# A hybrid decoder trunk: the decays of rows 512 to 1023 in two groups of two heads, and the minimum of their logits on VectorE

## The chip, the cores and the metric

One core of a Trainium2 chip. The metric is the time of one execution in microseconds (us) on the device, as the median of several runs. The engines are TensorE (PE in the profile, with its weight loads as PEld), VectorE (DVE), ScalarE (ACT), GpSimd (POOL) and the queue SP that issues the transfers (DMA). Matmuls write into eight PSUM banks of 128 x 512 fp32.

## The reference

One decoder layer over 1024 rows of 1024 columns. The normed input is projected once, and cut into q, k, v, z_a, a low-rank gate and the parts of a convolution branch. The part that matters here is the decay of the gated linear attention:

```python
gk = log_sigmoid(gk_low @ w_gk2 + b_gk) / 16        # (rows, 4 heads x 128)
b = cumsum(gk, within chunks of 64 rows)
q_in, k_in, k_dec = q * exp(b), k * exp(-b), k * exp(b_last - b)
```

With z = gk_low @ w_gk2 + b_gk, the log-sigmoid is min(z, 0) - ln(1 + exp(-|z|)). Beside it stand v, which the attention sums up, and z_a, which goes through Silu into a gate.

## The kernel before

Each wide projection (512 output columns for each 512-row half, with a contraction of 1024) is made of seven smaller products in the manner of Strassen. `wide` (L1339) takes two such blocks of columns, v and then za. Of each it runs products 3, 1, 2, 5, 4, 6 in this order, each 4 contraction tiles by 4 row blocks by 3 matmuls (the values are split into a high and a low fp32r part, `mm3`, L609): 48 matmuls of 128 x 512. Product 3 ends in four accumulators X; products 1 and 5 go into four accumulators V; products 2, 4 and 6 into Y. X and Y lie in the banks `first`, V in the banks `second`. For za, `first` is m4, m5 and two of the kind o, and `second` is m0 to m3. V is read by VectorE after product 5 (`zau <- zaV`), Y after product 4 (`zas <- zaY`).

The weights of a product are prepared by VectorE and ScalarE: raw tiles are loaded (`zaraw`, later q0raw, k0raw, q1raw, k1raw, all in 8 common buffers), combined (`zaT`), cast to the high part on ScalarE (`za6hi <- zaT`) and subtracted for the low part on VectorE (`za6lo`).

Into these products the kernel weaves side work, a step after each few matmuls (`weave`, `tick`, `finish_woven`, L617 to L632). Of it:

- `low_rank(half)` (L1513) makes the low-rank gate of one half of the rows, in a bank and then in a tile `low`.
- `decays(half, tags)` (L1534) does for each of four heads one matmul into a bank (`zp`), and from that bank two ScalarE operations: Relu(-z - b) into `c`, with a negated bias `nbgk`, and Abs(z + b) into `t`. Then follow Exp and Ln in place for all four heads, and for each head on VectorE the sum of both, a scan over the rows of a chunk, a subtraction and a tiny product (`dds`); scan and subtraction are stored.
- `quarter_sums(1)` (L1565) makes sums of the activations (`qs`), split and stored to `tqd`; they are loaded again later as `turned0h` and `turned0l` for the cells of q and k, in the matmuls `k0X <- turned0h` and `q0X <- turned0h`.
- `weights` prepares the weights of later projections (`wt`).

`extra` (L1604) runs the decays of rows 0 to 511 within v's products, through the argument `late` of `wide`, a function that `wide` calls ahead of product 4. `more` (L1610) runs those of rows 512 to 1023, in the banks m0 to m3, and `quarter_sums(1)` behind them; it is woven from the start of za on.

The order of the instructions isn't that of the code. All operations are recorded; each gets a due time, worked backward over what depends on it with estimated costs (`set_dues`, L373), and a list scheduler (`put_in_order`, L420) then takes, for each engine, the earliest due of those that are ready by its clock. The matmuls of the products stay in their order; side matmuls such as `zp` go in where their operands are ready and a bank is free. `emit` (L501) then issues everything, so all instructions have the line L508, and they are told apart by their names. Each engine runs its instructions in order, and so does SP; each transfer also waits for the one that is eight places before it.

Of the kernel before, what the change touches and what calls it, by code (L numbers as in the profile page):

```python
# [9 lines left out]
F32 = mybir.dt.float32  # L10
# [3 lines left out]
AF = mybir.ActivationFunctionType  # L14
ALU = mybir.AluOpType

P = 128
D = 1024
SEQ = 1024
HALF = 512  # L20
H = 4
DV = 256
CH = 64
NP = HALF // P
# [495 lines left out]
def kernel(  # L520
# [16 lines left out]
    nc = Flow(tc)  # L537
    PS = bass.MemoryType.PSUM
    tt = nc.vector.tensor_tensor
    stt = nc.vector.scalar_tensor_tensor  # L540
    act = nc.scalar.activation
# [21 lines left out]
    bgk = vec[:, 0:4]  # L563
# [8 lines left out]
    def dram(name, *shape):  # L572
        return dr.tile([P, *shape], F32, name=name)
# [5 lines left out]
    cd = [[[dram(f"c{w}d{h}_{i}", HALF) for w in "cd"] for i in range(2)] for h in range(H)]  # L579
# [16 lines left out]
    store = nc.sync.dma_start  # L596
# [6 lines left out]
    def mm(*a, **kw):  # L603
        nc.tensor.matmul(*a, skip_group_check=True, **kw)
# [12 lines left out]
    def weave(gen, after=1):  # L617
        woven.append([after, gen])
# [11 lines left out]
    def finish_woven():  # L630
        while woven:
            tick()  # L632
# [334 lines left out]
    def pairs(cs):  # L967
        for c in cs:
            c.prods = [k for k in PAIR if k in c.prods]
        return [list(cs[n:n + 2]) for n in range(0, len(cs), 2)]  # L970

    def run_groups(groups, more=(), ahead=6):


        todo = line_up(groups)
        seq = todo + line_up(more)
        for n, (c, k) in enumerate(todo):
            for reach, what in ((RING + ahead, "load"), (RING - 1, "prep")):
                met = set()
                for cc, kk in seq[n:]:  # L980
                    if cc not in met:
                        reach -= cc.slots
                    if cc.slots > 1:
                        met.add(cc)
                    if reach < 0 or not cc.ready(kk):
                        break
                    getattr(cc, what)(kk)
            c.run(k)
# [488 lines left out]
    with phase("v", [ph["prep0"]]) as qp:  # L1477
# [14 lines left out]
        smask = qp.tile([P, HALF], F32, name="smask")  # L1492
# [14 lines left out]
        nc.scalar.copy(g2, g2raw)  # L1507
        tt(g2[64:128], g2raw[64:128], f(g2[64:128]), op=ALU.subtract)
        lows = {}
        nbgk = qp.tile([P, 4], F32, name="nbgk")  # L1510
        nc.vector.tensor_scalar(nbgk, bgk, -1.0, None, op0=ALU.mult)

        def low_rank(half):  # L1513

            ops = ((0, 0), (4, 3)) if half == 0 else ((0, 1), (8, 6))
            glx = qp.tile([P, 8, 4, 32], F32R, tag="wt", name=f"glx{half}")
            for n, (g0, _) in enumerate(ops):
                nc.scalar.copy(glx[:, 4 * n:4 * n + 4], f(glw[:, g0:g0 + 4, None, :].to_broadcast([P, 4, 4, 32])))
            lowp = pso.tile([P, 512], F32, tag="o", name=f"lowp{half}", bufs=2)
            n = 0  # L1520
            for g0, k in ops:
                for kt in range(4):
                    gl = glx[:, n // 2].rearrange("p a b -> p (a b)")
                    for s in range(2):
                        nc.apart = 0.0 if n else 1.0
                        mm(lowp, gl, hres[k][s][:, kt, :], start=n == 0, stop=n == 15)
                        n += 1
            low = qp.tile([P, 512], F32R, tag="low", name=f"low{half}")
            nc.scalar.copy(low, lowp)
            for a in (32, 96):  # L1530
                tt(low[a:a + 32], lowp[a:a + 32], f(low[a:a + 32]), op=ALU.subtract)
            lows[half] = low

        def decays(half, tags):  # L1534
            t1 = [qp.tile([P, HALF], F32, tag="t1", name=f"t1_{half}{h}", bufs=4) for h in range(H)]
            c = [qp.tile([P, HALF], F32, tag="c4", name=f"c4_{half}{h}", bufs=4) for h in range(H)]
            for h in range(H):
                zp = pso.tile([P, 512], F32, tag=tags[h], name=f"zp{half}_{h}", bufs=2 if tags[h] == "o" else 1)
                cs = slice(h * P, (h + 1) * P)
                nc.apart = 1.0  # L1540
                mm(zp, g2[:, cs], lows[half], start=True, stop=True)
                nc.apart, nc.hurry = 0.0, 6.0
                act(c[h], zp, AF.Relu, scale=-1.0, bias=nbgk[:, h:h + 1])
                act(t1[h], zp, AF.Abs, bias=bgk[:, h:h + 1])
                nc.hurry = 0.0
                yield 1
            for t in t1:
                act(t, t, AF.Exp, scale=-1.0)
            for t in t1:
                act(t, t, AF.Ln, bias=1.0)  # L1550
            yield 1
            by = lambda t: t.rearrange("p (n c t) -> p n c t", c=2, t=CH)
            for h in range(H):
                tt(t1[h], t1[h], c[h], op=ALU.add)
                nc.vector.tensor_tensor_scan(c[h], smask, t1[h], 0.0, op0=ALU.mult, op1=ALU.add)
                store(cd[h][half][0], c[h])
                last = by(c[h])[:, :, :, CH - 1]
                tt(by(t1[h]), by(c[h]), by(c[h])[:, :, :, CH - 1:CH].to_broadcast([P, NP, 2, CH]), op=ALU.subtract)
                store(cd[h][half][1], t1[h])
                dc = dcs[:, h, half]  # L1560
                act(dc, last, AF.Exp, scale=-1 / 16.0)
                tt(dds[:, h, half], dc[:, :, 0], dc[:, :, 1], op=ALU.mult)
                yield 1

        def quarter_sums(k):  # L1565


            hi, lo = (f(t) for t in hres[k])
            at = lambda t, i, j: t[:, 2 * i:2 * i + 2, 256 * j:256 * j + 256]

            def tile(n):
                return qp.tile([P, 512], F32, tag="c4", name=f"qs{k}{n}", bufs=4).rearrange("p (a b) -> p a b", a=2)

            def apart(n, a, b):
                t, o = tile(n), tile("o")
                tt(t, at(hi, *a), at(hi, *b), op=ALU.subtract)
                tt(o, at(lo, *a), at(lo, *b), op=ALU.subtract)
                tt(t, t, o, op=ALU.add)
                return t

            def less(n, a, t):
                o = tile(n)
                tt(o, at(hi, *a), t, op=ALU.subtract)
                tt(o, o, at(lo, *a), op=ALU.add)
                return o

            def put(n, src):
                hl = [qp.tile([P, 512], F32, tag="t1", name=f"qs{k}{n}{w}", bufs=4).rearrange("p (a b) -> p a b", a=2) for w in "hl"]
                split(*(t.bitcast(F32R) for t in hl), src)
                for w, t in enumerate(hl):  # L1590
                    store(tqd[k][n][w], t)

            t = apart(0, (0, 1), (0, 0))
            put(0, t)
            yield 2
            t = less(1, (1, 1), t)
            put(1, t)
            yield 2
            put(3, less(3, (1, 0), t))
            yield 2  # L1600
            put(2, apart(2, (1, 1), (0, 1)))
            yield 2

        def extra():  # L1604
            low_rank(0)
            yield 2
            yield from decays(0, ("o",) * 4)
            low_rank(1)

        def more():  # L1610
            yield from decays(1, ("m0", "m1", "m2", "m3"))
            yield from quarter_sums(1)

        wide("v", [wv[0, n] for n in range(4)], v_cons, ("m0", "m1", "m2", "m3"), ("o", "o", "m4", "m5"),
             [(ep, "ev", 3)] * 2, [(ep, "ev", 3), (qp, "t1", 4)], begun, lambda: weave(extra(), 1))
        weave(more(), 1)
        weave(weights(qp, pieces[:3], 3, 5.0), 2)
        wide("za", [wv[1, n] for n in range(4)], z_cons, ("m4", "m5", "o", "o"), ("m0", "m1", "m2", "m3"),
             [(qp, "vhi", 2)] * 2, [(qp, "vlo", 2)] * 2)
        finish_woven()  # L1620
        qks = []
        for hp in range(2):
# [367 lines left out]
    with phase("late", [ph["sw"], ep]) as lp:  # L1990
# [57 lines left out]
        with phase("fin", [ph["sw4"]], lp) as gp:  # L2048
# [152 lines left out]
            last = pairs(gts)  # L2201
# [74 lines left out]
```

## Time and profile before

| what | value |
|---|---|
| median of 3 runs | 1072.09 us (1071.81 to 1072.77) |
| profiled execution | 1072.38 us |
| its span in the trace | 1070.5 us |
| mean granted TensorE clock | 0.998 |
| ScalarE table loads | 20, 1283 ns each |
| transfers | 262.06 MB |

In the lines of a timeline stand the start in us from the start of the span, the length, the engine, and the instruction with its tiles as output <- inputs, numbers left out; at the end in brackets the idle time of the engine ahead of it and whom it waited for. Lines that overlap are pipelined: the distance between two starts, the pitch, is what an instruction costs in a row of them. A line of the waits has the waiting instruction, the one waited for, the sum in us, how often, and the longest. A window has busy time and count of PE, PEld, DVE, ACT and POOL, the granted clock, the DMA share and GB/s. A group of a line has the total busy time and the mean ns. For a transfer the last number is the median time from issue to landing.

### The profile page before, as it was taken

What the parts mean: (1) busy time and instruction counts of PE and PEld (TensorE: products, weight loads), DVE (VectorE), ACT (ScalarE), POOL (GpSimd) and SP (SyncE); (2) the same over time, 40 slices, a digit from 0 to 9 for tenths busy, and PEclk for the clock granted to TensorE, in tenths of its full rate; (3) what the DMA queues carried; (4) which work ended last, traced back from release to release, by engine and by line L of the source; (5) the groups of instructions that cost most, each with busy time, mean ns of one, the idle gap of its engine ahead of it and who ended that gap; (6) DMA issues with size and microseconds to landing.
All of it is one profiled execution on the core that took longest, in us unless ns stands there. A gap on an engine that the chain in (4) does not pass through costs nothing.

```text
span 1070.5 us, 15921 instructions
## 1 busy us (share of the span) xinstructions
PE 1059.7 (99%) x5175; PEld 896.3 (84%) x5175; DVE 917.5 (86%) x1553; ACT 662.8 (62%) x1241; POOL 45.4 (4%) x83
## 2 busy tenths in 40 slices
PE   9999999999999999999999999999999999999996
PEld 7888887888888888888888888888888888888886
DVE  6889768977997888889889788887999879889896
ACT  6866689856654544566556376765856635466555
POOL 0000000000000000000000011110000000012021
PEclk9999999999999999999999999999999999999999
DMA  9985578785867443654557779978586779799973
GB/s 313 330 316 174 187 231 307 260 285 200 257 213 244 154 152 130 215 173 154 197 180 243 247 241 346 324 275 322 199 305 229 284 220 312 244 328 337 300 235 133
DMA packets 166979, 262.06 MB, mean 245 GB/s; under 512 B 14448, under 2 KB 79728, under 8 KB 163952
## 3 DMA queue, kind: packets, MB, share of 16 engines
q1 hardware_dynamic: 166752, 260.79, 72.1%
q8 instruction: 40, 0.66, 0.2%
q14 instruction: 43, 0.35, 0.1%
q10 hardware_dynamic: 144, 0.26, 0.1%
HBM read 168.72 MB, written 92.27 MB: 244 GB/s over the span
## 4 chain that ended last, share of the span: by engine, by line
PE 98%; ACT 1%; DMA 1%; DVE 0%; issue 0%; SPq 0%; POOL 0%; POOLq 0%; ACTq 0%
PE vY L508 3%; PE zaY L508 3%; PE vV L508 2%; PE op L508 2%; PE zaV L508 2%; PE pe L508 2%; PE zaX L508 1%; PE vzV L508 1%; PE vzX L508 1%; PE kv L508 1%; PE ga1Y L508 1%; PE ga0Y L508 1%; PE k0Y L508 1%; PE zc2Y L508 1%; PE zc1Y L508 1%; PE ga2Y L508 1%
## 5 line engine op out<-in xcount | busy, mean ns | idle before, releaser
L508 DVE TENSOR_TENSOR wt<-wt 128x256 f32<-128x256 f32 x64 | 26.9, 420 | 2.2 <-DMA wtd<-wt 1.9
L508 ACT ACT_TABLE_LOAD x20 | 25.7, 1283 | 1.1 <-PEq L2265 0.7
L508 DVE SCALAR_TENSOR_TENSOR u<-t,vec,u 128x512 f32<-128x512 f32 x32 | 23.8, 747 | 2.6 <-ACT u L508 2.5
L508 ACT ACTIVATE junk<-x 128x512 bf16<-128x512 f32 (+1 forms) x30 | 18.0, 600 | 12.0 <-DVE x L508 11.7
L508 POOL MEMSET t<- 128x2 f32 x8 | 0.8, 100 | 410.3 <-ACT kk L508 206.5
L508 POOL TENSOR_SCALAR rg<-ms 128x1 f32<-128x1 f32 x8 | 6.4, 798 | 261.6 <-ACT junk L508 261.4
L508 ACT ACTIVATE u<-t,vec 128x512 f32<-128x512 f32 x16 | 11.6, 726 | 7.9 <-issue 4.6
L508 ACT ACTIVATE junk<-op 128x256 bf16<-128x256 f32 x32 | 12.2, 380 | 3.8 <-PE op L508 3.7
L508 ACT ACTIVATE wt<-wt,vec 128x256 f32<-128x256 f32 x32 | 13.6, 497 | 1.0 <-DMA wt<-in_wb_dram 1.0
L508 ACT ACTIVATE og<-op,or 128x256 f32<-128x256 f32 x32 | 13.3, 470 | 1.2 <-POOL or L508 1.1
L508 ACT CAST S<-S 128x512 fp32r<-128x512 f32 x14 | 8.6, 617 | 8.7 <-PE op L508 7.5
L508 PE MATMUL pe<-wpehi,pThi 128*128 128x512 f32 x32 | 12.7, 398 | 0.6 <-ACT pThi L508 0.5
L508 ACT ACTIVATE oq<-oq,vec 128x512 f32<-128x512 f32 x20 | 13.1, 715 | 0.0
L508 PE MATMUL op<-v,aTh 128*128 128x256 f32 x64 | 12.8, 283 | 0.0
L508 PE MATMUL pe<-wpelo,pThi 128*128 128x512 f32 x32 | 12.7, 398 | 0.0
L508 DVE TENSOR_TENSOR szl<-og,szl 128x512 f32<-128x512 f32 x16 | 11.0, 687 | 2.0 <-ACT og L508 2.0
L508 PE MATMUL pe<-wpehi,pTlo 128*128 128x512 f32 x32 | 12.1, 393 | 0.0
L508 POOL TENSOR_TENSOR or<-or,mhalf 128x2 f32<-128x2 f32 x16 | 11.9, 746 | 1.3
L508 DVE SCALAR_TENSOR_TENSOR hq<-hq,vec,rt 128x512 f32<-128x512 f32 x16 | 11.4, 741 | 0.0
L508 DVE TENSOR_TENSOR s<-y,s 128x512 f32<-128x512 f32 x16 | 11.0, 686 | 0.5 <-ACT s L508 0.5
L508 POOL TENSOR_SCALAR or<-oms 128x2 f32<-128x2 f32 x16 | 5.6, 348 | 137.6 <-ACT junk L508 137.6
L508 DVE TENSOR_TENSOR x<-x,pe 128x512 f32<-128x512 f32 (+1 forms) x18 | 11.2, 629 | 0.3
(3671 smaller groups left out, 4333.7 us busy)
## 6 DMA issues: line engine op xcount, KB each, us to landing
wtd<-wt SPq DMA_DIRECT2D x88, 128.0 KB, 2.7
wt<-in_wb_dram SPq DMA_DIRECT2D x16, 512.0 KB, 4.5
v<-vd SPq DMA_DIRECT2D x16, 512.0 KB, 5.9
wgq<-wtd SPq DMA_DIRECT2D x7, 1024.0 KB, 6.6
qk<-qkd SPq DMA_DIRECT2D x12, 512.0 KB, 6.0
vraw<-in_wv_dram SPq DMA_DIRECT2D x20, 256.0 KB, 3.3
zaraw<-in_wv_dram SPq DMA_DIRECT2D x20, 256.0 KB, 4.4
uq<-ud SPq DMA_DIRECT2D x5, 1024.0 KB, 6.9
```

The costliest lines, as they stand in the source:

```text
L508: o.call(*[place(a) for a in o.args], **{k: place(a) for k, a in o.kw.items()})
```

## The change

In `decays`, VectorE adds the bias and takes the minimum with 0 in one operation that reads the bank, in place of ScalarE's Relu of the negated logit; the later sum becomes a difference. The negated bias isn't made any more. This holds for both halves of the rows. `decays` also gets the heads as an argument: of rows 512 to 1023 heads 0 and 1 stay in `more`, now in m0 and m1, and heads 2 and 3 are run in m2 and m3 by the function that `wide` calls ahead of za's product 4, when V has been read out of these banks.

```diff
-        nbgk = qp.tile([P, 4], F32, name="nbgk")
-        nc.vector.tensor_scalar(nbgk, bgk, -1.0, None, op0=ALU.mult)
...
-        def decays(half, tags):
-            t1 = [qp.tile([P, HALF], F32, tag="t1", name=f"t1_{half}{h}", bufs=4) for h in range(H)]
-            c = [qp.tile([P, HALF], F32, tag="c4", name=f"c4_{half}{h}", bufs=4) for h in range(H)]
-            for h in range(H):
+        def decays(half, heads, tags):
+            t1 = [qp.tile([P, HALF], F32, tag="t1", name=f"t1_{half}{h}", bufs=4) for h in heads]
+            c = [qp.tile([P, HALF], F32, tag="c4", name=f"c4_{half}{h}", bufs=4) for h in heads]
+            for n, h in enumerate(heads):
...
-                act(c[h], zp, AF.Relu, scale=-1.0, bias=nbgk[:, h:h + 1])
-                act(t1[h], zp, AF.Abs, bias=bgk[:, h:h + 1])
+                nc.vector.tensor_scalar(c[n], zp, bgk[:, h:h + 1], 0.0, op0=ALU.add, op1=ALU.min)
+                act(t1[n], zp, AF.Abs, bias=bgk[:, h:h + 1])
...
-                tt(t1[h], t1[h], c[h], op=ALU.add)
+                tt(t1[n], t1[n], c[n], op=ALU.subtract)
...
-            yield from decays(0, ("o",) * 4)
+            yield from decays(0, range(4), ("o",) * 4)
             low_rank(1)
 
         def more():
-            yield from decays(1, ("m0", "m1", "m2", "m3"))
+            yield from decays(1, range(2), ("m0", "m1"))
             yield from quarter_sums(1)
...
-             [(qp, "vhi", 2)] * 2, [(qp, "vlo", 2)] * 2)
+             [(qp, "vhi", 2)] * 2, [(qp, "vlo", 2)] * 2, None, lambda: weave(decays(1, range(2, 4), ("m2", "m3")), 1))
```

The order that the scheduler makes changes with it, up to about a third of the program; behind that the two orders are the same. Three places follow. In the rows a number behind a name tells tiles of one name apart; zp_2 and zp_3 are the decays' matmuls of heads 2 and 3.

TensorE at the end of za's product 3 and the start of product 1 (zaV), before:

```order
757 L508 MATMUL zaX_1815<-za3hi_1822,h3hi 128x512
758 L508 MATMUL zaX_1815<-za3lo_1847,h3hi 128x512
759 L508 MATMUL zaX_1815<-za3hi_1822,h3lo 128x512
760 L508 MATMUL zaV_2000<-za1hi_1864,h1hi 128x512
761 L508 MATMUL zp_3_2004<-low_1742,g_1407 128x512
762 L508 MATMUL zaV_2000<-za1lo_1880,h1hi 128x512
763 L508 MATMUL zaV_2000<-za1hi_1864,h1lo 128x512
764 L508 MATMUL zaV_2014<-za1hi_1864,h1hi 128x512
```

The last zp of rows 512 to 1023 stood within the first row block of V, and zp_2 eight rows ahead of it. Now TensorE has them a third into product 4 (zaY), which follows product 5:

```order
909 L508 MATMUL zaY_2028<-za4hi_2161,h4hi 128x512
910 L508 MATMUL zaY_2028<-za4lo_2193,h4hi 128x512
911 L508 MATMUL zaY_2028<-za4hi_2161,h4lo 128x512
912 L508 MATMUL zp_2_2374<-low_1759,g_1407 128x512
913 L508 MATMUL zaY_2086<-za4hi_2161,h4hi 128x512
914 L508 MATMUL zp_3_2382<-low_1759,g_1407 128x512
915 L508 MATMUL zaY_2086<-za4lo_2193,h4hi 128x512
```

Both stand around the fourth row block of the first contraction tile, after 9 and 10 of the 48 matmuls of product 4. On VectorE, what empties the banks ahead of them and reads them stands in this order now (zau empties V, c_12 and c_13 are the new operations of heads 2 and 3):

```order
267 L508 TENSOR_TENSOR k0T_2326<-k0raw_2225,k0raw_2217 128x512
268 L508 TENSOR_TENSOR qs12l<-qs_2263,qs12h 128x512
269 L508 TENSOR_TENSOR za6lo_2340<-zaT_1587,za6hi_2334 128x512
270 L508 TENSOR_TENSOR zau_2214<-zaV_1989,zau_2214 128x512
271 L508 TENSOR_TENSOR q0k00S_2351<-q0raw_2173,k0raw_2217 128x256
272 L508 TENSOR_TENSOR zau_2229<-zaV_1999,zau_2229 128x512
273 L508 TENSOR_TENSOR zau_2237<-zaV_2011,zau_2237 128x512
274 L508 TENSOR_TENSOR zau_2251<-zaV_2019,zau_2251 128x512
275 L508 TENSOR_SCALAR c_12_2380<-zp_2_2374,vec 128x512
276 L508 TENSOR_SCALAR c_13_2387<-zp_3_2382,vec 128x512
```

The four zau stand together, the third and fourth of them empty m2 and m3; before, the order had two of them ahead of the four zas and two behind the zas. Eleven rows later the first subtraction of head 2 (`t_12 <- t_12, c_12`) stands directly ahead of the four zas. The third place is SP, where the turned activations are loaded, now:

```order
220 L508 DMA q1raw_2531<-in_wc_dram 128x512
221 L508 DMA k1raw_2559<-in_wc_dram 128x512
222 L508 DMA q1raw_2566<-in_wc_dram 128x512
223 L508 DMA k1raw_2570<-in_wc_dram 128x512
224 L508 DMA q1raw_2577<-in_wc_dram 128x512
225 L508 DMA turned0h<-tqd_1h 128x512
226 L508 DMA turned0l<-tqd_1l 128x512
```

Before, only the first q1raw load and a store of zau stood ahead of these; four more loads do now. On ScalarE the eight Relu are gone, and there are three table loads more, since Exp and Ln of heads 2 and 3 now come apart from those of heads 0 and 1.

More of the change, by code (lines that the diff above doesn't have):

```diff
@@ L1532, in low_rank @@
             lows[half] = low
-        def decays(half, tags):
-            t1 = [qp.tile([P, HALF], F32, tag="t1", name=f"t1_{half}{h}", bufs=4) for h in range(H)]
-            c = [qp.tile([P, HALF], F32, tag="c4", name=f"c4_{half}{h}", bufs=4) for h in range(H)]
-            for h in range(H):
-                zp = pso.tile([P, 512], F32, tag=tags[h], name=f"zp{half}_{h}", bufs=2 if tags[h] == "o" else 1)
+        def decays(half, heads, tags):
+            t1 = [qp.tile([P, HALF], F32, tag="t1", name=f"t1_{half}{h}", bufs=4) for h in heads]
+            c = [qp.tile([P, HALF], F32, tag="c4", name=f"c4_{half}{h}", bufs=4) for h in heads]
+            for n, h in enumerate(heads):
+                zp = pso.tile([P, 512], F32, tag=tags[n], name=f"zp{half}_{h}", bufs=2 if tags[n] == "o" else 1)
                 cs = slice(h * P, (h + 1) * P)
@@ L1552, in decays @@
             by = lambda t: t.rearrange("p (n c t) -> p n c t", c=2, t=CH)
-            for h in range(H):
-                tt(t1[h], t1[h], c[h], op=ALU.add)
[L1555 to L1559, printed above, removed]
+            for n, h in enumerate(heads):
+                tt(t1[n], t1[n], c[n], op=ALU.subtract)
+                nc.vector.tensor_tensor_scan(c[n], smask, t1[n], 0.0, op0=ALU.mult, op1=ALU.add)
+                store(cd[h][half][0], c[n])
+                last = by(c[n])[:, :, :, CH - 1]
+                tt(by(t1[n]), by(c[n]), by(c[n])[:, :, :, CH - 1:CH].to_broadcast([P, NP, 2, CH]), op=ALU.subtract)
+                store(cd[h][half][1], t1[n])
                 dc = dcs[:, h, half]
```

## The prediction

> **What bounds the kernel.** I read the page first (engine shares, chain), then the waits of the whole run, then the timelines of TensorE and ScalarE around the one wait that matters. From the page, the span, the engines' busy time and the chain that ended last:
>
> ```profile
> span 1070.5 us, 15921 instructions
> PE 1059.7 (99%) x5175; PEld 896.3 (84%) x5175; DVE 917.5 (86%) x1553; ACT 662.8 (62%) x1241; POOL 45.4 (4%) x83
> PE 98%; ACT 1%; DMA 1%; DVE 0%; issue 0%; SPq 0%; POOL 0%; POOLq 0%; ACTq 0%
> ```
>
> TensorE is busy for 99% of the span and is 98% of the chain. So a change of the other engines' work is worth only the time in which TensorE waits. These are all of TensorE's waits in the run (total, times, longest):
>
> ```profile
> PE zaV L508 <- ACT t L508: 1.2, 2, 1.0
> PE warm L508 <- DVE zero L508: 1.0, 1, 1.0
> PE pe L508 <- ACT pThi L508: 0.5, 1, 0.5
> ```
>
> The last two lie at the start, where nothing is edited. The first is the place of the change. TensorE's timeline there (start, length, instruction; zp is the fourth head's decay matmul):
>
> ```profile
> 178.33 0.39 PE L508 MATMUL zp<-low,g 128*128 128x512 f32 x1
> ...
> 179.49 0.40 PE L508 MATMUL zaV<-za1hi,h1lo 128*128 128x512 f32 x1
> 180.86 0.50 PE L508 MATMUL zaV<-za1hi,h1hi 128*128 128x512 f32 x1 [0.98 <-ACT t L508]
> 181.20 0.40 PE L508 MATMUL zaV<-za1lo,h1hi 128*128 128x512 f32 x1
> 181.44 0.40 PE L508 MATMUL zaV<-za1hi,h1lo 128*128 128x512 f32 x1
> 182.02 0.51 PE L508 MATMUL zaV<-za1hi,h1hi 128*128 128x512 f32 x1 [0.18 <-ACT t L508]
> 182.36 0.40 PE L508 MATMUL zaV<-za1lo,h1hi 128*128 128x512 f32 x1
> ```
>
> And ScalarE's in the same microseconds:
>
> ```profile
> 178.08 1.58 ACT L508 ACTIVATE sz<-zaX 128x512 f32<-128x512 f32 x3
> 179.53 0.70 ACT L508 ACTIVATE c<-zp,nbgk 128x512 f32<-128x512 f32 x1
> 180.10 0.71 ACT L508 ACTIVATE t<-zp,vec 128x512 f32<-128x512 f32 x1
> 180.67 0.72 ACT L508 ACTIVATE c<-zp,nbgk 128x512 f32<-128x512 f32 x1
> 181.24 0.73 ACT L508 ACTIVATE t<-zp,vec 128x512 f32<-128x512 f32 x1
> ```
>
> Row block 2 of V needs bank m2, which holds the third head's zp until its Abs (`t<-zp`, 180.10) has read it; row block 3 needs m3, held until the Abs at 181.24. Both stand behind three Silu of `sz` and the Relu (`c<-zp`). TensorE follows each Abs at once.
>
> **What goes.** The undisturbed pitch of a matmul comes from two anchors, the first matmul of product 5 and the first of product 6, 96 matmuls apart; the third head's zp stands with them:
>
> ```profile
> 176.48 0.39 PE L508 MATMUL zp<-low,g 128*128 128x512 f32 x1
> ...
> 201.88 0.39 PE L508 MATMUL zaV<-za5hi,h5hi 128*128 128x512 f32 x1
> ...
> 223.64 0.39 PE L508 MATMUL zaY<-za6hi,h6hi 128*128 128x512 f32 x1
> ```
>
> (223.64 − 201.88)/96 = 0.227 us. From 179.49 to 182.36 there are 5 steps in 2.87 us, where 5 × 0.227 = 1.13 would do: **1.74 us** lost. After the change heads 2 and 3 aren't in m2 and m3 at all at this time. Were the banks free? The zp of heads 2 and 3 themselves started in them at 176.48 and 178.33 without waiting, and V wants them no earlier than 179.7, so what used them before is gone 1.4 us or more ahead. The whole 1.74 us goes at this place; no other wait of TensorE is near the edit, so nothing more than that can be gained.
>
> **What is added, and its cover.** Eight Relu leave ScalarE (8 × 0.57, the pitch of 179.53 to 180.10, = 4.6 us), three table loads come. Eight VectorE operations from a bank come, a small one (nbgk) leaves. The trace has no such TENSOR_SCALAR. Its bounds are the two-input operation from the bank (0.69 long, 0.60 from one to the next) and, below, the 128x256 operation (0.42 long); I take 0.60, since the bank and the 512 columns are those of the first row. Neither engine is on the chain, so these cost nothing as long as the following cover holds. VectorE, from the `vs` that ends its long wait at 149.77 to the first `zau` (window, then rows and groups):
>
> ```profile
> 149.77:216.51 66.74, 65.58 (x286) 53.23 (x285) 61.30 (x104) 60.59 (x101) 0.00 (x0) 1.00 0.81 270
> ```
>
> ```profile
> 216.51 0.69 DVE L508 TENSOR_TENSOR zau<-zaV,zau 128x512 f32<-128x512 f32 x1
> ...
> 221.99 1.88 DVE L508 TENSOR_TENSOR zas<-zaY,zas 128x512 f32<-128x512 f32 x3
> ```
>
> ```profile
> L508 DVE TENSOR_TENSOR_SCAN c<-smask,t 128x512 f32<-128x512 f32 x8 | 9.8, 1219 | 0.0
> ...
> L508 DVE TENSOR_TENSOR wt<-wt 128x256 f32<-128x256 f32 x12 | 5.1, 421 | 0.0
> ```
>
> The pitch is (1.88 − 0.69)/2 = 0.60, so 0.09 less than the length; for the scan 1.13, for `wt` 0.33. Between these two points the new order lacks the later work of heads 2 and 3 (2 × (0.60 + 1.13 + 0.60) = 4.7), three `wt` (1.0) and one za3lo (0.6), together 6.3; it has two new bank operations, q0T, k0T and a qs12l in addition, 5 × 0.60 = 3.0. Busy time 61.3 − 3.3 = 58.0, so the first `zau` starts at 207.8 with no idle time, and at 213.2 with the same 5.4 us idle as before.
>
> What it must meet: zp of head 2 now stands in TensorE's order nine matmuls into product 4, in m2, and V's third block in m2 is released by the third `zau`. Product 5 starts at 201.88 − 1.74 − 0.45 (two zp gone from ahead) = 199.69; zp of head 2 is due 57 × 0.227 = 12.9 later, **212.6**. On the way to the first `zau` VectorE waits for the third cast of za6, whose buffer product 5 must have read. ScalarE's rows:
>
> ```profile
> 210.24 0.62 ACT L508 CAST za6hi<-zaT 128x512 fp32r<-128x512 f32 x1 [1.46 <-PE zaV L508]
> ...
> 215.94 0.62 ACT L508 CAST qs12h<-qs 128x512 fp32r<-128x512 f32 x1
> 216.58 1.28 ACT L508 ACT_TABLE_LOAD   x1
> 217.87 1.15 ACT L508 ACTIVATE zau<-zau 128x512 f32<-128x512 f32 x2
> ```
>
> That is 8.36 after product 5's start, so 208.05 now; with the cast (0.62) and za6lo (0.60) the first `zau` is at **209.3**, between the two ends, and nearer to the lower one. The third ends 2.2 later (0.60 + 0.33 + 0.60 + 0.69), at 211.5, the fourth at 212.1. Cover: 1.1 us at zp of head 2, 1.0 at head 3's.
>
> Then the second cover. In VectorE's order the first subtraction of head 2 now stands ahead of the four `zas`, which free the banks for product 6 (due 98 × 0.227 = 22.2 after 199.69, **221.9**). The subtraction waits for ScalarE: from 212.1 a Silu 0.57, a cast 0.53, a Silu 0.57, a cast 0.53, two Abs 1.14, a table load 1.29 (216.58 to 217.87), two Exp 1.14, a load 1.29, one Ln 0.66: 219.8; subtraction 0.60, first `zas` 0.69: 221.1. Cover 0.8 us.
>
> The Trainium skill, "PSUM — Partial Sum Buffer", section "PSUM bank collisions raise a hardware error", says that VectorE and ScalarE may not read one bank at a time and that the compiler orders them, so the minimum and the Abs of a head would take turns. No run here shows it; by it the bank is held for an estimated 1.4 us, no longer than by Relu and Abs.
>
> **Queues passed.** SP's order changes with the buffers: the second k0raw load and the six loads of the turned activations.
>
> ```profile
> 201.87 0.42 SPq L508 DMA_DIRECT2D k0raw<-in_wc_dram  x1
> ...
> 227.31 0.86 SPq L508 DMA_DIRECT2D q1raw<-in_wc_dram  x1
> ...
> 229.37 0.32 SPq L508 DMA_DIRECT2D turned0h<-tqd_1h  x1
> ```
>
> ```profile
> k0raw<-in_wc_dram SPq DMA_DIRECT2D x4, 256.0 KB, 5.9
> ...
> turned0h<-tqd_1h SPq DMA_DIRECT2D x1, 256.0 KB, 5.3
> ...
> turned0l<-tqd_0l SPq DMA_DIRECT2D x1, 256.0 KB, 6.2
> ```
>
> ```profile
> L508 PE MATMUL k0X<-turned0h,q0k00Shi x2: 279/280/282, 242.7 to 243.0; 128*128 128x256 f32 x2
> ...
> L508 PE MATMUL q0X<-turned0h,q0k00Shi x2: 281/281/281, 244.1 to 244.5; 128*128 128x256 f32 x2
> ```
>
> Even if k0raw is issued no earlier than before, it lands at 207.8; k0T, qs12l and za6lo follow and the first `zau` comes at 209.6 instead of 209.3. The turned loads land 5.3 to 6.2 after issue, so the first had 8 us to spare. They now stand behind five loads of q1raw and k1raw instead of one, and I work out below what this takes.
>
> **Sum.** The profiled execution took 1072.38 us (span 1070.5 and 1.88 around it): 1072.38 − 1.74 = 1070.64. It is 0.29 above the median of the runs shown, 1072.09, so on the median 1070.35, **1070.4**. That is −0.16%. A measurement of this kernel can tell about 0.2%, 2.1 us, from no change.
>
> **Rival A, slower: TensorE waits for VectorE at the moved zp.** TensorE works in order; if the third `zau` is late, zp of head 2 and all of product 4 behind it stand still. For it: VectorE has 5.4 us idle in that window before, of which I let most vanish, and both covers are 1 us. Against it: the waits of before come from ScalarE's full queue, which gets shorter. With all of that idle time kept, the first `zau` is at 213.2, the third ends at 215.4: 2.8 us of waiting; the chain to `zas` shifts by 3.9 against 2.8 + 0.8 of cover, 0.3 more. 3.1 − 1.74 = +1.4: 1073.5. With `zau` where it was, 216.51, the waits are 6.1 + 0.3: 1076.8. It beats the gain when the first `zau` starts later than 212.1, and measurably from about 214.3.
>
> **Rival B: the turned loads come late.** The last raw load ahead of them needs a buffer that the second k0T frees, and that now stands behind q0k00Blo, which VectorE ran here:
>
> ```profile
> 232.48 0.43 DVE L508 TENSOR_TENSOR q0k00Blo<-k0raw,q0k00Bhi 128x256 fp32r<-128x256 f32 x1 [0.60 <-ACT q0k00Bhi L508]
> ```
>
> That is 8.84 after product 6's start; with its 0.33, a q0T (0.60) and the k0T (0.69) the buffer is free 10.5 after it, at 232.4. Then the loads start at 233 to 235, the later ones up to 237 with the pending transfers, and land between 238.6 and 243. They are needed 19.1 and 20.5 after product 6's start (242.7 and 244.1 against 223.64), 241.0 and 242.4. A wait of 0 to 1.5 us: 1070.4 to 1071.9, at the middle 1071.1.
>
> **Rival C: table loads cost more than their row.** Two of them now lie in the chain to `zas`. In the trace the cast ahead ends at 216.56, the load starts at 216.58 and the Silu follows 1.29 later. If 1.38 came on top of each, `zas` would end at 223.9, 2.0 after it is wanted: 1072.4. The Trainium skill, "ScalarE: Activation LUTs", section "What ACT_TABLE_LOAD costs", has 1.28 us for the load and about 1.38 more for emptying the engine. The trace agrees with the first and shows 0.02 for the second.
>
> **Rival D: the wait stays.** Something other than Relu and Abs would hold m2 and m3: 1072.1. Against it speaks the free start of both zp.
>
> **Chances.** Forecast 0.55, A 0.20, B 0.13, C 0.04, D 0.08. Somewhat over half of A, where VectorE is later than with the idle time of before, lies above 1074.2: slower 0.11. Faster by over 0.2% needs a median under 1069.95; the sum doesn't reach it, but the runs of before scatter from 1071.81 to 1072.77, so I give a quarter of the forecast's cases, 0.13. The rest, 0.76, is within 0.2%. The range goes from 1069.7 (the sum and a good half-microsecond of scatter) to 1073.5, which takes in B, C, D and A with the idle time of before; 0.12 lies above, some 0.07 below.
>
> **What would show it.** Right: no wait of zaV for ScalarE's `t`; product 5 starts near 199.7; zp of heads 2 and 3 start at 212.6 and 213.1 with no idle time; first `zau` at 209.3; first `zas` near 220.4; product 6 at 221.9. Wrong: a wait `zp <- DVE zau` or `zaY <- DVE zas` (A, C), `k0X` or `q0X` waiting for a DMA (B), zaV still waiting (D), or a TENSOR_SCALAR from the bank longer than 0.75 us.

## The result, and the profile after

| | median (us) | runs | ratio to before, 95% interval |
|---|---|---|---|
| before | 1072.26 | 9 | |
| changed | 1069.73 | 9 | 0.9975 (0.9967 to 0.9984) |
| forecast | 1070.4 | | 0.9984 |

The changed kernel is 2.5 us faster, 0.25%. The place and the kind of the gain are as forecast; the size is not, and it falls just on the other side of the 0.2% at which "no change" ended.

From the page of the changed kernel, span, engines and ScalarE's table loads, and the only row that is left of TensorE's waits:

```profile
span 1067.5 us, 15922 instructions
PE 1058.9 (99%) x5175; PEld 896.9 (84%) x5175; DVE 922.9 (86%) x1560; ACT 661.5 (62%) x1236; POOL 45.3 (4%) x83
L508 ACT ACT_TABLE_LOAD x23 | 29.5, 1283 | 1.2 <-PEq L2263 0.7
```

```profile
PE warm L508 <- DVE zero L508: 1.0, 1, 1.0
```

VectorE is 5.4 us busier, ScalarE 1.3 us less busy, and neither shows. TensorE at the start of the third and the fourth row block of V, where it stood still before, and at the two zp that were moved:

```profile
178.17 0.39 PE L508 MATMUL zaV<-za1hi,h1lo 128*128 128x512 f32 x1
178.39 0.39 PE L508 MATMUL zaV<-za1hi,h1hi 128*128 128x512 f32 x1
...
179.07 0.39 PE L508 MATMUL zaV<-za1hi,h1hi 128*128 128x512 f32 x1
...
211.49 0.40 PE L508 MATMUL zaY<-za4hi,h4lo 128*128 128x512 f32 x1
211.72 0.39 PE L508 MATMUL zp<-low,g 128*128 128x512 f32 x1
211.95 0.40 PE L508 MATMUL zaY<-za4hi,h4hi 128*128 128x512 f32 x1
212.18 0.39 PE L508 MATMUL zp<-low,g 128*128 128x512 f32 x1
...
221.07 0.39 PE L508 MATMUL zaY<-za6hi,h6hi 128*128 128x512 f32 x1
```

Every step is 0.23 us now. VectorE's rows that were to meet these times (the group of three zau is the second, third and fourth):

```profile
208.47 0.69 DVE L508 TENSOR_TENSOR zau<-zaV,zau 128x512 f32<-128x512 f32 x1
209.07 0.42 DVE L508 TENSOR_TENSOR q0k00S<-q0raw,k0raw 128x256 f32<-128x256 f32 x1
209.40 1.88 DVE L508 TENSOR_TENSOR zau<-zaV,zau 128x512 f32<-128x512 f32 x3
212.15 1.41 DVE L508 TENSOR_SCALAR c<-zp,vec 128x512 f32<-128x512 f32 x2 [0.86 <-PE zp L508]
...
219.36 0.69 DVE L508 TENSOR_TENSOR t<-t,c 128x512 f32<-128x512 f32 x1 [2.13 <-ACT t L508]
219.97 2.48 DVE L508 TENSOR_TENSOR zas<-zaY,zas 128x512 f32<-128x512 f32 x4
```

The third zau ends at 210.00 + 0.69 = 210.69, 1.03 us ahead of zp of head 2; the first zas at 220.66, 0.41 ahead of product 6. And the turned activations: the issue of the last load, its time to landing, and its first reader of the second group:

```profile
235.65 0.43 SPq L508 DMA_DIRECT2D turned0l<-tqd_0l  x1
```

```profile
turned0l<-tqd_0l SPq DMA_DIRECT2D x1, 256.0 KB, 5.8
```

```profile
241.66 0.28 PE L508 MATMUL q0X<-turned0l,q0k00Shi 128*128 128x256 f32 x1
```

It lands at 241.45, 0.2 us before it is read: rival B's cover is used up, and just holds.

Where the 3.1 us between the two traces lie comes from the first starts of a few matmuls in each trace. The table also has the experiments told below (in us; "to end of span" goes to the last instruction in the trace, where the expectations below have 8.28 and 7.84 from spans given to 0.1 us; "load" is the last load of instructions, counted from the last matmul, found in windows of 0.05 us):

| kernel | to first vV | to za's product 3 | to q0V | to last matmul | to end of span | load |
|---|---|---|---|---|---|---|
| before | 103.29 | 63.09 | 68.14 | 827.70 | 8.33 | 8.05 |
| before_again | 102.80 | 63.09 | 68.15 | 827.68 | 8.26 | 8.00 |
| changed | 102.63 | 62.99 | 66.33 | 827.71 | 7.82 | 9.35 |
| after_again | 103.02 | 62.99 | 66.32 | 827.93 | 7.82 | 9.35 |
| split_only | 102.62 | 62.99 | 66.66 | 827.74 | 8.32 | 8.10 |
| min_only | 102.76 | 63.45 | 68.69 | 827.69 | 8.24 | 8.00 |
| vec_late2 | 102.54 | 62.99 | 67.57 | 828.35 | 7.84 | 9.35 |
| vec_late4 | 103.35 | 62.99 | 70.27 | 827.71 | 7.88 | 9.40 |
| before_dve20 | 102.52 | 63.10 | 68.12 | 827.68 | 8.32 | 8.05 |
| after_sp4 | 102.91 | 62.98 | 66.33 | 827.79 | 8.12 | 8.40 |
| after_sp8 | 102.90 | 62.99 | 66.32 | 836.55 | 8.16 | 7.90 |
| before_sp_less | 102.59 | 63.12 | 68.10 | 827.69 | 8.00 | 6.50 |
| turned_first | 102.84 | 62.98 | 66.33 | 827.74 | 7.83 | 8.80 |

Three pieces of before against changed: 0.66 up to the first matmul of v's V, where nothing was edited; 0.10 + 1.81 = 1.91 around the edit; 0.51 behind the last matmul, where the instructions are the same too. Of the 0.51, 0.06 is the landing of the last store (6.92 and 6.86 after the last matmul) and 0.45 lies behind it.

### The profile page after: what moved, and what is told of

The parts are those of the page before. It is cut to its first block, busy times and chain, and to the rows that moved or that the text cites. A ratio compares the mean times of both kernels' runs of the same rounds, so it can differ in the third digit from the quotient of the medians.

```text
span 1067.5 us, 15922 instructions
## 1 busy us (share of the span) xinstructions
PE 1058.9 (99%) x5175; PEld 896.9 (84%) x5175; DVE 922.9 (86%) x1560; ACT 661.5 (62%) x1236; POOL 45.3 (4%) x83
## 4 chain that ended last, share of the span: by engine, by line
PE 99%; ACT 0%; DVE 0%; issue 0%; POOL 0%; POOLq 0%
PE vY L508 3%; PE zaY L508 3%; PE pe L508 2%; PE vV L508 2%; PE zaV L508 2%; PE op L508 2%; PE zaX L508 1%; PE vzV L508 1%; PE vzX L508 1%; PE kv L508 1%; PE ga1Y L508 1%; PE ga0Y L508 1%; PE k0Y L508 1%; PE cc3Y L508 1%; PE cc2Y L508 1%; PE zc0Y L508 1%
```

## The experiments

**Which of the pieces repeat.** Both kernels once more, unchanged.

> The kernel before, unchanged, for a second trace and more times. Theory S (stage): the change is worth 1.9 us, all of it between the start of za's product 3 and q0V; the 0.66 us by which the changed kernel's trace was ahead already at 102 us and the 0.44 us by which its end is shorter are scatter from one execution to the next. Then the ratio is within 0.1% of 1, the two waits of zaV for ScalarE stay (1.2 us by the waits, 1.74 lost), and the times before the first product of v (103.29 in the first trace) and after the last matmul (8.28) differ from the first trace by some tenths of a us. Theory R (rest): the change shortens the start and the end as well; then both come out within 0.1 us of the first trace of before.

> The changed kernel, unchanged, for a second trace and more times. Theory S: the ratio is between 0.9970 and 0.9985, about 0.9980 with many rounds (1.9 us of 1072), product 3 of za to q0V again takes 66.3 us against 68.1, and the time up to the first product of v and after the last matmul moves by some tenths against its first trace. Theory R: again 0.9975 or less, and again 102.6 us and 7.8 us at start and end.

Measured: before_again 1072.03, ratio 0.9997 (0.9988 to 1.0006); after_again 1069.89, ratio 0.9979 (0.9971 to 0.9988). The start is scatter: 103.29 and 102.80 of one kernel, 102.63 and 103.02 of the other. The stage is the same to 0.01 us within each kernel, 1.91 and 1.93 apart. But the end is not scatter, as theory S had it: 8.33 and 8.26 of one kernel, 7.82 twice of the other, and behind the landing of the last store 1.41 and 1.40 against 0.96 twice, 0.44 apart. So 1.91 + 0.44 = 2.35 us are the change's, between the 2.2 and 2.5 of the medians. Theory R was right on the end and wrong on the start.

**Which half of the edit takes the wait.** The groups alone, and the minimum alone:

```diff
 split_only, against the changed kernel (nbgk is made again, as before)
-                nc.vector.tensor_scalar(c[n], zp, bgk[:, h:h + 1], 0.0, op0=ALU.add, op1=ALU.min)
+                act(c[n], zp, AF.Relu, scale=-1.0, bias=nbgk[:, h:h + 1])
...
-                tt(t1[n], t1[n], c[n], op=ALU.subtract)
+                tt(t1[n], t1[n], c[n], op=ALU.add)
 min_only, against the changed kernel
-            yield from decays(1, range(2), ("m0", "m1"))
+            yield from decays(1, range(4), ("m0", "m1", "m2", "m3"))
...
-             ..., None, lambda: weave(decays(1, range(2, 4), ("m2", "m3")), 1))
+             ...)
```

> The two groups of heads alone; ScalarE keeps the Relu. Theory S: what takes the wait away is that heads 2 and 3 leave m2 and m3, so zaV has no wait for ScalarE here either, and product 3 of za to q0V takes 66.3 to 66.6 us; time within 0.4 us of the changed kernel. Theory M (minimum): the shorter ScalarE queue takes the wait away; then a wait of over 1 us stays somewhere near zaV or zp, and the time is within 0.6 us of the kernel before.

> VectorE's minimum alone; all four heads stay together in m0 to m3. Theory S: the two Abs of heads 2 and 3 still stand behind three Silu (the order has two copies between them besides), so zaV waits for about 0.7 us at m2 and 0.8 us at m3, 1.5 lost against 1.74, and the time is 0 to 0.6 us below the kernel before. Theory M: without Relu the banks come free 0.6 and 1.1 us sooner and most of the wait goes, 1.1 us or more below the kernel before.

split_only took 1070.62, ratio 0.9984 (0.9975 to 0.9993): the groups take the wait away. It is 0.73 above the changed kernel of the same session, where theory S had at most 0.4: by the traces its end is 0.50 longer, of which more below, and its stage 0.33. The trace shows where most of the 0.33 starts, at product 6 (TensorE, then VectorE):

```profile
220.86 0.39 PE L508 MATMUL zaY<-za4hi,h4lo 128*128 128x512 f32 x1
221.27 0.47 PE L508 MATMUL zaY<-za6hi,h6hi 128*128 128x512 f32 x1
221.57 0.39 PE L508 MATMUL zaY<-za6lo,h6hi 128*128 128x512 f32 x1
```

```profile
219.23 1.29 DVE L508 TENSOR_TENSOR t<-t,c 128x512 f32<-128x512 f32 x2 [2.52 <-ACT t L508]
220.44 2.48 DVE L508 TENSOR_TENSOR zas<-zaY,zas 128x512 f32<-128x512 f32 x4
```

The first zas ends at 221.13 and product 6 starts at 221.27, 0.18 later than at the usual pitch. The two Relu in ScalarE's queue are not what delays it: the first subtraction starts at 219.23 here and at 219.36 in the changed kernel. But the order has a second subtraction ahead of the zas, 0.60 more, and that uses up the second cover. So the run shows the price of this order; a price of the Relu at this place it doesn't show.

min_only took 1074.07, ratio 1.0013 (1.0005 to 1.0022): slower than before, where I had put it slightly faster. Its rows, TensorE's and ScalarE's:

```profile
180.79 0.50 PE L508 MATMUL zaV<-za1hi,h1hi 128*128 128x512 f32 x1 [1.07 <-ACT t L508]
...
182.41 0.50 PE L508 MATMUL zaV<-za1hi,h1hi 128*128 128x512 f32 x1 [0.66 <-ACT t L508]
```

```profile
178.58 1.57 ACT L508 ACTIVATE sz<-zaX 128x512 f32<-128x512 f32 x3
180.03 0.70 ACT L508 ACTIVATE t<-zp,vec 128x512 f32<-128x512 f32 x1
180.60 1.13 ACT L508 COPY zaY<-zax 128x512 f32<-128x512 f32 x2
181.63 0.72 ACT L508 ACTIVATE t<-zp,vec 128x512 f32<-128x512 f32 x1
```

With no Relu in the queue the scheduler has put two copies between the two Abs, as the order said, and the second bank comes free no sooner than before. Product 1 with its zp takes 13.43 us instead of 12.90. A wait that the kernel before doesn't have stands in v's product 2, where a weight load (PEld) waits for ScalarE's copies; it costs 0.46 us:

```profile
115.30 0.19 PEld L508 LDWEIGHTS vY<-v2hi,h2hi 128*128 128x128 f32 x1 [0.57 <-ACT vY L508]
```

Together the way from the first vV to q0V is 0.91 us longer than before. That fits the five executions of 1072.42 to 1073.24, with a mean granted clock of 0.998 or 0.999; the profiled one, 1072.62, is of these. The other six, and the median with them, took 1074.07 to 1074.85 at 0.996. So some 1.5 us more go with the lower clock; at which place it fell isn't shown, since none of the six has a trace. The next experiment shows such a stretch in a trace.

**What a late VectorE costs (rival A).** Work is repeated on VectorE directly ahead of the first zau, in the place where the order has it:

```diff
 vec_late4, against the changed kernel (vec_late2 has 3 in place of 5)
-                o.call(*[place(a) for a in o.args], **{k: place(a) for k, a in o.kw.items()})
+                for _ in range(5 if o.engine == DVE and o.name.startswith("za6lo2<-") else 1):
+                    o.call(*[place(a) for a in o.args], **{k: place(a) for k, a in o.kw.items()})
```

> The changed kernel with the low part of the third weight tile of product 6 computed five times instead of once, directly ahead of the first zau: VectorE is 4 x 0.60 = 2.4 us later there. By the covers of the prediction's rival A (in the changed kernel's trace the third zau ends 1.03 us before the zp of head 2, the first zas 0.41 us before product 6 needs it), TensorE waits 1.4 us at zp of head 2 for VectorE and some 0.6 us more at the start of product 6: 2.0 us above the changed kernel, about the time of the kernel before. If the banks' cover isn't the limit (VectorE catches up, or TensorE can run other work), under 0.5 us.

> As the run with VectorE 2.4 us late, but 1.2 us late (the low part of the third weight tile of product 6 computed three times). By the covers (1.03 us at zp of head 2, 0.41 us at zas) TensorE waits 0.2 us at zp and 0.6 us at product 6: 0.8 us above the changed kernel. Theory C (clock): the run with 2.4 us cost 3.94 us in its trace because TensorE's granted clock fell to 0.54 for 3.5 us behind a wait of 1.94; waits under 1 us leave the clock alone, so here no stretch has a granted clock under 0.9 and the executions lie within 1 us of each other. If a late VectorE costs twice its wait in any case, 1.6 us or more above the changed kernel.

vec_late4 took 1072.73, ratio 1.0007 (0.9998 to 1.0016), 2.9 us above the changed kernel. Six of its eleven executions took 1072.04 to 1072.73, five 1073.53 to 1074.06; the trace is of the slowest. In it TensorE waits for VectorE at zp, and then runs slowly:

```profile
212.21 0.39 PE L509 MATMUL zaY<-za4hi,h4lo 128*128 128x512 f32 x1
214.53 0.50 PE L509 MATMUL zp<-low,g 128*128 128x512 f32 x1 [1.94 <-DVE zau L509]
214.87 0.39 PE L509 MATMUL zaY<-za4hi,h4hi 128*128 128x512 f32 x1
215.13 0.63 PE L509 MATMUL zp<-low,g 128*128 128x512 f32 x1
215.55 0.63 PE L509 MATMUL zaY<-za4lo,h4hi 128*128 128x512 f32 x1
```

The windows of that stretch and of the next (the granted clock is the third column from the end):

```profile
215.10:218.60 3.50, 3.50 (x10) 2.72 (x10) 3.50 (x7) 3.48 (x8) 0.00 (x0) 0.54 0.73 255
218.60:222.00 3.40, 3.40 (x16) 2.80 (x15) 1.59 (x5) 3.37 (x4) 0.00 (x0) 0.98 0.39 130
```

At a granted clock of 0.54 nine steps from 215.13 to 218.88 take 3.75 us where 9 x 0.227 = 2.04 would do: 1.71 us behind a wait of 2.1. So in this execution the wait cost almost twice its length, 3.94 of stage; the six faster ones, 2.2 to 2.9 us above the changed kernel, have by their times not paid all of it. vec_late2 took 1071.17, ratio 0.999 (0.9981 to 0.9999), about 1.4 above the changed kernel, where 0.8 was expected. Its wait at zp is 0.5 us, the granted clock is 1.00 in every window from 205 to 228 us of its trace, and its stage is 1.24 longer: 0.9 at zp with its restart, the rest at product 6. In addition the turned load was late, 0.2 us by the waits and 0.6 between q0V and the last matmul:

```profile
PE zp L509 <- DVE zau L509: 0.5, 1, 0.5
PE q0X L509 <- DMA turned0l<-tqd_0l: 0.2, 1, 0.2
```

Both waits at zp are longer than expected (1.94 for 1.4, 0.5 for 0.2), because the repeats cost more than 0.60 each. VectorE's rows, of vec_late2 and of vec_late4:

```profile
207.96 2.14 DVE L509 TENSOR_TENSOR za6lo<-zaT,za6hi 128x512 fp32r<-128x512 f32 x3
```

```profile
208.75 3.59 DVE L509 TENSOR_TENSOR za6lo<-zaT,za6hi 128x512 fp32r<-128x512 f32 x5
```

That is 0.73 from one to the next. Counted from the start of product 5, the first zau is 1.64 and 3.07 later than in the changed kernel; less the cover of 1.03 this leaves 0.61 and 2.04, and zp is 0.66 and 2.09 late. So rival A's mechanism is shown and its cover at zp is as read. Of theory C the clock is borne out: it fell behind the wait of 1.94 us and stayed up behind the one of 0.5. Its time, 0.8 above the changed kernel, isn't. The Trainium skill, "TensorE: Matmul & The Clock Gate", section "HAM oscillation — how this bites in real kernels", puts the idle gap that lowers the clock at about 3.4 us; here a wait of 1.94 was enough.

**The end of the program.** Both kernels issue their last two stores at the same distance from the last matmul (1062.22 before, 1059.66 changed), and by the profile's rows these take equally long:

```profile
1066.31 0.40 ACTq L508 DMA_DIRECT2D out_dram<-x  x1
```

```profile
1063.74 0.39 ACTq L508 DMA_DIRECT2D out_dram<-x  x1
```

```profile
out_dram<-x ACTq DMA_DIRECT2D x1, 256.0 KB, 2.8
```

So all but the 0.06 of the landing is in the closing, behind it. The page has one difference that lies there: the queue that loads instructions, before and changed:

```profile
q14 instruction: 43, 0.35, 0.1%
```

```profile
q14 instruction: 42, 0.34, 0.1%
```

The last load lies 0.25 us ahead of the end of the span before, and 1.5 us behind it in the changed kernel. The four kernels here lengthen or shorten one engine's stream, in places with time to spare:

```diff
 after_sp4, after_sp8 (changed kernel): the first row of a wtd store ("last") again, 4 or 8 times
...
+                for _ in range(4 if o is last else 0):
+                    o.call(*[a[0:1] for a in args], **{k: a[0:1] for k, a in kw.items()})
...
 before_dve20 (kernel before): the last dds, 21 times
...
+                for _ in range(21 if o is last else 1):
...
 before_sp_less (kernel before): 12 stores of szd ("moved") from ScalarE's queue
...
+                call = self.scalar.real.dma_start if o in moved else o.call
```

> The changed kernel with eight more instructions on SP, behind the last store of wtd: the first row of it (1 KB) stored again eight times. In four traces a load of instructions (queue q14) lies 0.25 to 0.5 us ahead of the end of the span and the end comes 8.2 to 8.3 us after the last matmul; in both traces of the changed kernel that load comes 1.5 us after the span and the end at 7.84. Theory F (fetch): SP's stream (1554 instructions with their extra waits in the changed kernel, 1558 to 1563 in the others) sets where that load falls. Then here, with 1562, the load is back ahead of the end, the end 8.2 to 8.3 us after the last matmul, and the time 0.4 us above the changed kernel. If VectorE's stream sets it (2273 against 2253 to 2268), or the end is shorter for another reason, it stays at 7.84.

> The kernel before with twenty more instructions on VectorE: the last dds of rows 512 to 1023 (0.08 us each, in a stretch where VectorE has idle time) is done 21 times instead of once, so VectorE's stream has 2274 instructions with their extra waits, as the changed kernel has. If VectorE's stream sets where the last load of instructions falls, the end comes 7.84 us after the last matmul and the time is 0.4 us below the kernel before. If SP's does (theory F as put for the run beside), the end stays at 8.28 and the time within 0.1% of the kernel before; the two waits of zaV stay in both.

> The changed kernel with four more instructions on SP, in a stretch where SP waits 6 us for its next transfer: the first row of one wtd store (1 KB) stored four times more. SP's stream has 1558 instructions with their extra waits, as many as the kernel with the groups alone, whose last load of instructions lay ahead of the end. Theory F: the load is back ahead of the end, the end comes 8.2 to 8.3 us after the last matmul, nothing else moves, and the time is 0.4 us above the changed kernel (0.9983 of the kernel before). Else: 7.84 and the changed kernel's time.

> The kernel before with twelve stores (the Silu of za: four zau, four zas and the last four sz) issued from ScalarE's queue instead of SP's, so that SP's stream has 1546 instructions with their extra waits. Theory F: the last load of instructions moves behind the end, the end comes 7.84 us after the last matmul, and the time is 0.4 us below the kernel before (ratio 0.9996), with the two waits of zaV in place. Else 8.28 and a ratio of 1.0 or above (ScalarE has twelve issues more).

before_dve20: end 8.32, 1072.22, ratio 1.0 (0.9991 to 1.0009). VectorE's stream doesn't set it. after_sp4: end 8.12, 1070.13, ratio 0.9982 (0.9974 to 0.9991), all else as in the changed kernel. before_sp_less: end 8.00, 1071.72, ratio 0.9996 (0.9987 to 1.0005), its waits of zaV in place. after_sp8: end 8.16, but 1078.77: TensorE waited 5.4 us for VectorE's `s` late in the program and the mean clock was 0.994, so only its end counts. That its small stores held up transfers there is likely, but not shown.

So edits of SP's stream move the end by 0.3 us in both directions. The form that I gave theory F fails, though: in after_sp4 the load is still 0.3 us behind the end, and in before_sp_less it comes 1.5 us ahead of the end rather than behind it. The traces also list SP's own instructions, and these show where the time goes. In the kernel before, SP pauses once in the closing, from 7.10 to 7.44 us after the last matmul, where the changed kernel has 0.04 between the same two instructions; and the drain behind the pause takes 130 ns instead of 7. SP's drains, before and changed (shortest, median and longest in ns):

```profile
L2272 SPq DRAIN  x3: 7/7/130, 1069.7 to 1070.1; - x3
```

```profile
L2270 SPq DRAIN  x3: 7/7/7, 1066.7 to 1067.0; - x3
```

The traces list 1492 instructions of SP before and 1485 in the changed kernel (the counts in the expectations are higher; no trace shows them). Seven traces have 1489 to 1494: the three of the kernel before's order (before, before_again, before_dve20), split_only, min_only, after_sp4 and after_sp8. In each of them a pause of 0.33 to 0.36 us stands ahead of the 1488th, whichever instruction that is. Six traces have 1471, 1485 or 1486, and none of them has the pause. So the changed kernel's end is shorter because its stream stops three instructions short of that place. In after_sp4 the pause meets the last drain, and the end is 0.30 longer rather than 0.44; before_sp_less has no pause, and its end is 8.00 rather than 7.82 because its last store lands 0.18 later.

The load of instructions isn't what SP waits for: it starts 0.97 to 0.99 us after the pause begins, when SP is already running again. What SP waits for there stays open.

**A version that beats both.** Rival B's cover in the changed kernel is 0.2 us, and in after_again's trace the last turned load landed 0.1 us too late (827.93 between q0V and the last matmul, 0.2 more than elsewhere). So the six loads were put ahead of the last four raw loads on SP:

```diff
+            at = [n for n, o in enumerate(order) if o.engine == SP and o.name.startswith("turned0")]
+            raws = [o for o in order[:at[0]] if o.engine == SP and o.name.startswith(("q1raw", "k1raw"))][-4:]
+            order = ([o for o in order[:at[5] + 1] if o not in raws] + raws + order[at[5] + 1:])
```

> The changed kernel with the six loads of the turned activations issued ahead of the four raw loads that stand before them on SP. In the changed kernel's two traces the last turned load lands 0.2 us ahead of and 0.1 us behind its first reader (q0X). Rival B's cover: with the loads about 2 us earlier it lands 2 us ahead, q0X waits in no execution, and from q0V to the last matmul it takes 827.7 us in the trace; the median is 0.1 to 0.2 us below the changed kernel, 1069.7 (ratio about 0.9977), which the interval can't tell from it. If the raw loads, now 2 us later, are then late for q1 and k1 (first read at 249.7 in the kernel before), a wait of q1V takes the gain back: 0.5 us or more above the changed kernel.

1069.56, ratio 0.9973 (0.9963 to 0.9984), TensorE has no wait but the one at the start. The last turned load, its time to landing and the same reader as above:

```profile
231.88 0.46 SPq L511 DMA_DIRECT2D turned0l<-tqd_0l  x1
```

```profile
turned0l<-tqd_0l SPq DMA_DIRECT2D x1, 256.0 KB, 5.5
```

```profile
241.86 0.28 PE L511 MATMUL q0X<-turned0l,q0k00Shi 128*128 128x256 f32 x1
```

The cover is 4.5 us instead of 0.2 (2 expected), and no raw load is late for it. The time can't be told from the changed kernel's; the trace says that a hazard is gone.

## Why the prediction was wrong, and where it was right

- **What bounds the kernel, and the wait:** right. Both waits of zaV were caused by heads 2 and 3 standing in m2 and m3 behind ScalarE's queue; split_only shows it.
- **The added operations:** the minimum from the bank takes 0.75 us and 0.66 from one to the next, where I took 0.69 and 0.60; it is just at the 0.75 that I had named as a sign of being wrong, and without effect. In the rows of the changed kernel and of min_only, taken in order, the minimum and the Abs of one head don't overlap, and one Abs waited 0.28 us for its minimum (head 0 of rows 0 to 511 in the changed kernel, at 143.68).
- **The covers:** read in distances from the start of product 5 (198.79 in this trace), zp of head 2 comes at 12.93 (12.9 forecast), the first zau at 9.68 (9.6), the first zas at 21.18 (20.7), product 6 at 22.28 (22.2). Cover at zp 1.03 for 1.1, at zas 0.41 for 0.8.
- **Rival B:** issue at 233.1 to 235.7 (233 to 237 forecast), landing at 241.45, need at 241.66. The mechanism is there, at zero to 0.2 us here.
- **Rival A:** mechanism and cover right, price too low. I priced the wait by its length; the trace of vec_late4 shows that the clock can add almost as much again.
- **Rivals C and D:** neither came. The first table load in the chain to zas starts at 214.94 and takes 1.28 us in the changed kernel, and the next operation starts at 216.23; no wait of zaV is left.
- **The step that failed:** "The whole 1.74 us goes at this place; no other wait of TensorE is near the edit, so nothing more than that can be gained." It is the cap. The stage gave 1.91, 0.17 more. About 0.1 of that is a step that I didn't see because I listed TensorE's waits for its matmuls alone: in the kernel before, a weight load in v's product 6 waited for VectorE, whose `vs` stood behind the decays of rows 0 to 511, and one step between two matmuls there took 0.32 us instead of 0.227 (that product 11.01 us, and 10.89 in the changed kernel).

```profile
156.73 0.19 PEld L508 LDWEIGHTS vY<-v6hi,h6hi 128*128 128x128 f32 x1 [0.24 <-DVE vs L508]
```

In the changed kernel this `vs` comes 0.33 us sooner and the wait is gone. The rest, some 0.07, is in the steps behind side matmuls, 0.23 to 0.24 instead of 0.227, which are fewer (not tried what sets them). And the end gave 0.44, SP's pause, which no list of TensorE's waits shows, since it lies behind the last matmul. 1.74 + 0.17 + 0.44 = 2.35 us, 0.22%, is over the bound of 2.1 us, and so the 0.13 for "faster" was far too low: I had taken the terms that I couldn't see as zero, and had left only scatter for them. That the end fell to the side of the gain is luck: it hangs on the length of SP's stream, which the edit didn't aim at. Without it the gain would have stayed within the bound.

## What to carry to other kernels

When TensorE is nearly all of the chain, read the wait that is left and move what holds its bank, not only the work ahead of it in the queue: here the shorter queue alone gained nothing, the other place of the two heads nearly all. List the waits of the weight loads beside those of the matmuls. A wait that may take the old one's place can cost more than its length: the one of 1.94 us was followed by 3.5 us at about half the clock. And where the forecast lies near the bound of what can be measured, a term of some tenths outside the list of waits decides the verdict, so the chance of the other side must not rest on the sum alone.

## What the runs showed of the hardware

- Behind a wait of 1.94 us TensorE's granted clock was 0.54 for 3.5 us and the pitch of its matmuls 0.43 instead of 0.227 us (vec_late4's trace).
- SP paused for 0.33 to 0.36 us ahead of its 1488th instruction, in seven traces whose streams have 1489 to 1494, at five different instructions of the closing; six traces with shorter streams have no such pause. With it the program ended 8.12 to 8.33 us after the last matmul, without it 7.82 to 8.00.
- A VectorE operation with one bank as its input, a per-partition bias and a minimum took 0.75 us for 128x512, against 0.69 for the two-input operation from a bank.
- The same VectorE subtraction of 128x512, repeated on the same tiles, took 0.73 us from one to the next (vec_late2, vec_late4), where operations of this length on different tiles took 0.60.
